# Last routing steps of a mixture-of-experts layer moved to other places in the order, and their padding matmuls with them

## The chip, the core and the metric

The kernel runs on one core of a Trainium2 chip. The metric is the device time of one execution in microseconds (us). Five engines work from queues of their own: PE (TensorE, matmuls; PEld is its weight load), DVE (VectorE), ACT (ScalarE), POOL (GpSimd) and SP (SyncE, which here issues nearly all transfers). They wait for each other through semaphores.

## The reference, cut to what matters

One decoder layer over 1024 tokens of width 1024, in fp32:

```python
proj = x @ w_in                              # split into 9 parts
y_a = hgrn2(hq, hf, hi, hg, ...) @ w_branch_a
y_b = sliding_window_attention(aq, ak, av, sinks) @ w_branch_b
merged = sigmoid(ga) * y_a + sigmoid(gb) * y_b
x = layer_norm(alpha * x + merged @ w_out, ln1_g, ln1_b)
# experts: best of 4 groups, then the best 2 of its 8 experts; 32 experts in all
glog = x @ w_rg + b_rg
elog_sel = (x @ w_re + b_re)[group of glog.max]
weights = softmax(glog)[group] * softmax(top2(elog_sel))
y[t] = sum over the 2 experts e of t:  weight * (silu(x @ w_gate[e]) * (x @ w_up[e])) @ w_down[e]
x = layer_norm(alpha * x + y, ln2_g, ln2_b)
```

## The kernel before

The work falls into four stretches: projections and attention, the recurrence, the mixing with `w_out`, the norm and the router (`mixing`, to about 811 us), and the loop over 32 experts (`moe`, 820 to about 1430 us) with the last norm. Every fp32 product is made of three matmuls on split operands: each operand is cast to fp32r on ACT (`h`, line 94), and DVE subtracts the cast from the original to get the rest (`l`, line 95). `mm3` then issues lines 99 (h with h), 100 and 101.

**The mixing stretch** is written out in ticks, two for each of 32 blocks `main`. A block's first half runs in an even tick, its second half in the odd one. Blocks 24 to 31 project the token tiles 4 to 7 with `w_out`, two column halves c each, 24 matmuls a block. What follows a tile (norm, router) is entered for later ticks. The router works on two tiles at a time (a batch) in five steps: `turn` (transposes, line 910, copied by ACT, line 912), `logits` (line 919, copied by ACT with the bias, line 920), `choose` (transposes on line 935, then a chain of small DVE operations that ends in `asg`, line 955), `place` (ranks on PE, lines 975 and 977, then DVE lines 981 to 997 up to `rat`) and `enter` (line 1004, into one table in PSUM). `BATCHES` holds for each batch the distance in ticks from a tile's norm to each step. `choose`, `place` and `enter` come last in their tick. `warm` issues matmuls on constants that nobody reads, so many in a tick as `WARM` says; each shows as two rows in the trace. After the last tick `slots` turns the table into indices (line 1018), issues the first two gathers and 20 more such matmuls; then all engines branch on a count (line 1297), and `moe` begins.

**The expert loop** streams the weights in pieces of 512 KB, 12 an expert: four of `w_g`, four of `w_u`, four of `w_d`; the order is `w_g` and `w_u` of expert e+1, then `w_d` of expert e. Piece n is loaded into an `er` tile by `fetch`, cast by ACT to `eh` and subtracted by DVE to `el` (`halve`) three pieces ahead of PE, and used in six matmuls by `piece`. `turn_x` transposes the gathered tokens of an expert (line 1097) and splits them into `xh` and `xl`; `turn_h` transposes the product of the two first layers (line 1115). Both write into the same two PSUM banks `pb`, so `turn_h` must wait until DVE has made `xl` from a bank. The order of instructions on each engine is that of the code.

All `er`, `eh` and `el` tiles, and the tiles of `w_out` before them, come from one pool of 36 buffers (`NQ`). The addresses in the built program show that buffers are handed out in the order in which they came free. A new tile waits for the last reader of the tile that had its buffer.

How many pieces are loaded ahead of the loop is set by the mixing stretch: ten are fetched in blocks 24 to 30, and then `fetch(True)` runs at the end of every tick from 62 on, four times at two ticks and twice at each later one, up to `NRAW` = 29 in all. In the loop each piece fetches one more, so this distance stays.

```python
            if tick >= 2 * len(main) - 1:
                for _ in range(4 if tick < 2 * len(main) + 1 else 2):
                    self.fetch(True)
```

Of the kernel before, what the change touches and what calls it, by code (L numbers as in the profile page):

```python
# [57 lines left out]
class Builder:  # L58
# [52 lines left out]
            for _ in range(n):  # L111
                self.nc.tensor.matmul(ps[:, 0:128], self.c("ident"), self.c("ident"), start=True, stop=True)

    WARM = {63: 11, 66: 15, 67: 5}

    def pe_order(self):
        return self.tc.manual_schedule(engines={mybir.EngineType.PE})
# [602 lines left out]
    def mixing(self):  # L720
# [84 lines left out]
        def norm(b, i, t, mv):  # L805
            for c in range(2):
                self.scale(t, mv, g1, b1, c)
            self.at(b + 2 * (i < 7), lambda: store(i, t))
            batch = next(g for g in self.BATCHES if i in g[0])
            if i == batch[0][0]:  # L810
# [8 lines left out]
        def store(i, t):  # L819
            for d in (self.x1d, self.zd):  # L820
                nc.sync.dma_start(d[i * 128:i * 128 + 128, :], t)
# [26 lines left out]
        while tick < 2 * len(main) or stages or self.late_stages:  # L848
# [15 lines left out]
            for fn in self.late_stages.pop(tick, []):  # L864
                fn()
            self.warm(self.WARM.get(tick, 0))
            tick += 1
# [23 lines left out]
    def small(self, n, nm, bufs=1):  # L891
        return self.tile([128] + (list(n) if isinstance(n, tuple) else [n]), F32, "r" + nm, bufs)

    BATCHES = ((0, 1), (4, 5, 6, 10, 14)), ((2, 3), (4, 5, 6, 10, 14)), ((4, 5), (2, 3, 4, 8, 9)), ((6, 7), (2, 3, 3, 4, 5))

    def router(self, batch):

# [536 lines left out]
```

## Time and profile before

| | |
|---|---|
| median of 3 runs | 1482.07 us (1479.93 to 1483.83) |
| time of the profiled execution | 1479.16 us |
| its span, first to last instruction | 1477.3 us |
| busy in the span: PE, PEld, DVE, ACT, POOL | 95%, 79%, 71%, 55%, 12% |
| mean granted TensorE clock | 0.988 of full speed |

The busy shares are means over stretches of different kinds. A matmul's end is modelled in these profiles, and matmuls overlap, so a busy PE is not PE at its peak; a pause of PE is nevertheless a pause.

### The profile page before, as it was taken

To read this page: it belongs to the slowest core of one execution; us is meant where nothing else is said; L and a number is where in the kernel's file an instruction comes from. 1 tells how busy PE (TensorE), PEld (TensorE's weight loads), DVE (VectorE), ACT (ScalarE), POOL (GpSimd) and SP (SyncE) were. 2 spreads that over 40 slices of the span, in tenths; PEclk is the share of its full clock that TensorE was granted. 3 is DMA by queue.
4 is the path that set the end of the run, shared out by engine and by line. 5 is a ranking of instruction groups with operands and counts; after the bars stand their busy time and mean duration, and the time that the engine had idled before them with its cause. 6 is when DMAs were issued, how large, how long until landed. Compare 5 with 4: busy or idle time off the path is not lost. (4 is left out here: it accounts for less than half of the span.)

```text
span 1477.3 us, 21008 instructions
## 1 busy us (share of the span) xinstructions
PE 1400.5 (95%) x7466; PEld 1172.5 (79%) x7466; DVE 1055.1 (71%) x1680; ACT 811.3 (55%) x1236; POOL 183.3 (12%) x137
## 2 busy tenths in 40 slices
PE   7999999999999999999997999999999999999992
PEld 5888899998888888788787877777777777777771
DVE  3266654647656764867645788888888888888978
ACT  3367434324443443313101777787777777877865
POOL 0000000000000000410000111111111111111125
PEclk9999999999999999999998999999999999999997
DMA  6124322344334323874538799999999999999643
GB/s 227 57 87 141 110 72 79 101 136 131 101 107 150 93 93 100 251 238 150 204 139 320 274 350 348 355 350 352 352 361 353 358 353 355 356 361 368 232 153 114
DMA packets 157726, 326.17 MB, mean 221 GB/s; under 512 B 18421, under 2 KB 79093, under 8 KB 157616
## 3 DMA queue, kind: packets, MB, share of 16 engines
q1 hardware_dynamic: 148688, 308.78, 58.2%
q0 software_dynamic: 8928, 16.00, 4.5%
q8 instruction: 60, 0.98, 0.3%
q14 instruction: 50, 0.41, 0.1%
HBM read 289.86 MB, written 51.38 MB: 231 GB/s over the span
## 5 line engine op out<-in xcount | busy, mean ns | idle before, releaser
L95 DVE TENSOR_TENSOR el<-er,eh 128x1024 fp32r<-128x1024 f32 x384 | 464.5, 1222 | 73.3 <-ACT eh L94 42.5
L94 ACT CAST eh<-er 128x1024 fp32r<-128x1024 f32 x384 | 395.5, 1050 | 105.2 <-PE mm L100 54.1
L100 PE MATMUL mm<-el,xh 128*128 128x512 f32 x512 | 202.9, 396 | 0.0
L101 PE MATMUL mm<-eh,xl 128*128 128x512 f32 x512 | 202.6, 396 | 0.0
L99 PE MATMUL mm<-eh,xh 128*128 128x512 f32 x512 | 201.5, 393 | 0.0
L99 PE MATMUL mm<-xh,wh 128*128 128x512 f32 x480 | 198.5, 414 | 0.0
L101 PE MATMUL mm<-xh,wl 128*128 128x512 f32 x480 | 188.7, 393 | 0.0
L100 PE MATMUL mm<-xl,wh 128*128 128x512 f32 x480 | 186.9, 389 | 0.0
L99 PEld LDWEIGHTS mm<-eh,xh 128*128 128x128 f32 x512 | 96.1, 188 | 23.6
L100 PEld LDWEIGHTS mm<-el,xh 128*128 128x128 f32 x512 | 96.1, 188 | 23.5
L101 PEld LDWEIGHTS mm<-eh,xl 128*128 128x128 f32 x512 | 96.1, 188 | 22.5
L101 PEld LDWEIGHTS mm<-xh,wl 128*128 128x128 f32 x480 | 90.0, 188 | 20.4
L99 PE MATMUL mm<-eh,hth 128*128 128x512 f32 x256 | 105.4, 412 | 0.7 <-ACT hth L94 0.7
L99 PEld LDWEIGHTS mm<-xh,wh 128*128 128x128 f32 x480 | 90.4, 188 | 15.4 <-DVE xl L95 0.4
L100 PEld LDWEIGHTS mm<-xl,wh 128*128 128x128 f32 x480 | 90.6, 189 | 14.7
L101 PE MATMUL mm<-eh,htl 128*128 128x512 f32 x256 | 101.3, 396 | 0.0
L100 PE MATMUL mm<-el,hth 128*128 128x512 f32 x256 | 100.2, 391 | 0.0
L1037 POOL DMA_INDIRECT xg<-x1d,gi x32 | 55.7, 1739 | 310.6 <-PE pb L1097 282.5
L1041 POOL DMA_INDIRECT zd<-y,gi x30 | 58.5, 1950 | 197.1 <-ACT y L1166 179.9
L99 PE MATMUL mm<-wh,xh 128*128 128x256 f32 x256 | 74.1, 290 | 0.0
L101 PE MATMUL mm<-wh,xl 128*128 128x256 f32 x256 | 72.4, 283 | 0.0
L100 PE MATMUL mm<-wl,xh 128*128 128x256 f32 x256 | 72.4, 283 | 0.0
(248 smaller groups left out, 2536.3 us busy)
## 6 DMA issues: line engine op xcount, KB each, us to landing
er<-w_g SPq DMA_DIRECT2D x128, 512.0 KB, 6.9
er<-w_u SPq DMA_DIRECT2D x128, 512.0 KB, 5.6
er<-w_d SPq DMA_DIRECT2D x128, 512.0 KB, 7.3
wr<-w_in SPq DMA_DIRECT2D x38, 512.0 KB, 4.7
gated<-st SPq DMA_DIRECT2D x32, 256.0 KB, 2.1
st<-gated SPq DMA_DIRECT2D x32, 256.0 KB, 3.3
x<-x SPq DMA_DIRECT2D x8, 512.0 KB, 9.3
wab<-w_a SPq DMA_DIRECT2D x16, 256.0 KB, 4.1
```

The costliest lines, as they stand in the source:

```text
L94: self.nc.scalar.copy(hi, src)
L95: (eng or self.nc.vector).tensor_sub(lo, src, hi.bitcast(F32))
L99: mm(out, lh, rh, start=start, stop=False)
L100: mm(out, lh, rl, start=False, stop=False)
L101: mm(out, ll, rh, start=False, stop=stop)
L1037: self.nc.gpsimd.indirect_dma_start(self.xg[e % 2], None, self.x1d, bass.IndirectOffsetOnAxis(ap=self.gi[:, e:e + 1], axis=0), bounds_chec ...
L1041: self.nc.gpsimd.indirect_dma_start(self.zd, bass.IndirectOffsetOnAxis(ap=idx, axis=0), y, None, bounds_check=T - 1, oob_is_err=False, com ...
```

## The change

Two tables change. The batch of tiles 4 and 5 does `place` and `enter` two ticks sooner, which puts them inside the last block of `w_out`; the batch of tiles 6 and 7 does all its steps one tick sooner; and the padding matmuls are spread over four ticks (31 of them before, 35 now).

```diff
-    WARM = {63: 11, 66: 15, 67: 5}
+    WARM = {63: 11, 65: 5, 66: 14, 67: 5}
...
-    BATCHES = ((0, 1), (4, 5, 6, 10, 14)), ((2, 3), (4, 5, 6, 10, 14)), ((4, 5), (2, 3, 4, 8, 9)), ((6, 7), (2, 3, 3, 4, 5))
+    BATCHES = ((0, 1), (4, 5, 6, 10, 14)), ((2, 3), (4, 5, 6, 10, 14)), ((4, 5), (2, 3, 4, 6, 7)), ((6, 7), (1, 2, 2, 3, 4))
```

On PE, at the last block of `w_out` (rows 99 to 101 on `mh` and `ml` are its matmuls; `rasg` and `rsum` belong to `place` of tiles 4 and 5, row 919 to `logits` of tile 6):

```order
 L919 MATMUL pa<-rxT,wr 36x128 x8
-L112 MATMUL mm<-const 128x128 x11
 L975 MATMUL pa<-rasg,const 128x32
 L977 MATMUL pa<-rsum,const 128x32
 L975 MATMUL pa<-rasg,const 128x32
 L977 MATMUL pa<-rsum,const 128x32
+L99 MATMUL mm<-h,mh 128x512
+L100 MATMUL mm<-l,mh 128x512
+L101 MATMUL mm<-h,ml 128x512
```

The second half of the last block (twelve matmuls, of which three are shown) stood ahead of these rows and now follows them. In the built program the first row of line 975 waits for ACT as well as for DVE, because ACT's copy of the logits reads the same bank.

On PE just behind it, from `enter` of tiles 4 and 5 through `turn`, `logits` and `choose` of tile 7 (`u` is the normed tile):

```order
 L1004 MATMUL tb<-rpay,rat 128x64 x4
+L112 MATMUL mm<-const 128x128 x11
 L910 MATMUL pb<-const,u 128x128 x8
-L112 MATMUL mm<-const 128x128 x15
+L112 MATMUL mm<-const 128x128 x5
 L919 MATMUL pa<-rxT,wr 36x128 x8
 L935 MATMUL pa<-const,rlT 128x36 x2
-L112 MATMUL mm<-const 128x128 x5
+L112 MATMUL mm<-const 128x128 x14
```

The real steps keep their order; most of the padding behind `turn` moved: eleven matmuls stand ahead of `turn` now, and fourteen instead of five behind the transposes of `choose`. On DVE, `place` of tiles 4 and 5 (lines 981 to 997) moves in the same way from behind the last tile's norm (lines 875 to 883) to ahead of its second half's addition (line 797).

The batch of tiles 6 and 7 ends one tick sooner, so there is one tick less at whose end pieces are fetched: 28 are under way ahead of the loop instead of 29. SP's queue has one load less ahead of the branch and one more behind it. With that, the buffers that the tiles of the loop take are others. On ACT, one expert's casts around its `xh`, before, with what each waits for beside its load:

```order
L94 CAST eh<-er 128x1024 [waits DMAHW2_49,DVE_49]
L94 CAST eh<-er 128x1024 [waits DMAHW3_49,PE_49]
L94 CAST eh<-er 128x1024 [waits DMAHW4_49,DVE_49]
L94 CAST xh<-pb 128x512 [waits DMASW3_49,PE_49]
L94 CAST xh<-pb 128x512 [waits PE_49]
```

and in the changed program:

```order
L94 CAST eh<-er 128x1024 [waits DMAHW2_49,DVE_49,PE_49]
L94 CAST eh<-er 128x1024 [waits DMAHW3_49,DVE_49,PE_49]
L94 CAST eh<-er 128x1024 [waits DMAHW4_49,DVE_49,PE_49]
L94 CAST xh<-pb 128x512 [waits DMASW3_49,PE_49]
L94 CAST xh<-pb 128x512 [waits PE_49]
```

The addresses tell which tile had the buffer. Before, the cast of piece n usually takes the buffer of the raw piece n-2, and the subtraction that of the `el` of n-4, which PE must have used; but once an expert, at the first piece of `w_g` (the second row above), the cast itself takes the `el` of n-4. That is the first piece of `w_d` of the expert before. Now the cast of piece n usually takes the buffer of the `eh` of n-5, and the subtraction that of the raw piece n-2; at the first piece of `w_g` the cast takes the `eh` of n-5 too, and the subtraction the `el` of n-4.

On DVE, the same place before (the second row belongs to the first piece of `w_g`):

```order
L95 TENSOR_TENSOR el<-er,eh 128x1024 [waits DMAHW2_49,PE_49,Activation_49]
L95 TENSOR_TENSOR el<-er,eh 128x1024 [waits DMAHW3_49,DVE_49,Activation_49]
L1153 TENSOR_TENSOR hh<-hh,mm 128x512 [waits PE_49]
L95 TENSOR_TENSOR el<-er,eh 128x1024 [waits DMAHW4_49,PE_49,Activation_49]
L95 TENSOR_TENSOR xl<-pb,xh 128x512 [waits DMASW5_49,Activation_49]
```

and now:

```order
L95 TENSOR_TENSOR el<-er,eh 128x1024 [waits DMAHW2_49,DVE_49,Activation_49]
L95 TENSOR_TENSOR el<-er,eh 128x1024 [waits DMAHW3_49,PE_49,Activation_49]
L1153 TENSOR_TENSOR hh<-hh,mm 128x512
L95 TENSOR_TENSOR el<-er,eh 128x1024 [waits DMAHW4_49,DVE_49,Activation_49]
L95 TENSOR_TENSOR xl<-pb,xh 128x512 [waits DMASW5_49,Activation_49]
```

The wait for PE has moved from the usual subtraction to the one at the first piece of `w_g`.

## Rows read from the trace of the kernel before

**Rows 1.** Busy time by engine in one expert's stretch; last PE clock, DMA share, GB/s.

```profile
core 0: us, PE busy (x) PEld busy (x) DVE busy (x) ACT busy (x) POOL busy (x), PEclk, DMA share, GB/s
900.00:919.20 19.20, 18.33 (x85) 14.79 (x84) 16.75 (x17) 15.29 (x18) 3.55 (x2) 1.00 0.98 366
```

**Rows 2.** Who waited for whom, expert loop (820 to 1400): total, times, longest.

```profile
ACT eh L94 <- PE mm L100: 54.1, 33, 1.8
...
PE pb L1115 <- DVE xl L95: 25.3, 29, 0.9
```

**Rows 3.** Timeline of one expert: start, us, engine, line; in brackets idle and releaser.

```profile
1042.11 0.63 PE L1115 MATMUL pb<-const,hh 128*128 128x128 f32 x4 [0.87 <-DVE xl L95]
...
1056.08 0.39 PE L100 MATMUL mm<-el,hth 128*128 128x512 f32 x1
...
1056.51 2.00 ACT L94 CAST eh<-er 128x1024 fp32r<-128x1024 f32 x2 [1.80 <-PE mm L100]
...
1057.58 1.23 DVE L95 TENSOR_TENSOR el<-er,eh 128x1024 fp32r<-128x1024 f32 x1 [1.17 <-ACT eh L94]
...
1058.41 1.06 ACT L94 CAST xh<-pb 128x512 fp32r<-128x512 f32 x2
...
1059.33 1.22 DVE L95 TENSOR_TENSOR el<-er,eh 128x1024 fp32r<-128x1024 f32 x1
...
1060.02 0.40 PE L101 MATMUL mm<-eh,htl 128*128 128x512 f32 x1
...
1060.46 1.28 DVE L95 TENSOR_TENSOR xl<-pb,xh 128x512 fp32r<-128x512 f32 x2
...
1061.29 0.63 PE L1115 MATMUL pb<-const,hh 128*128 128x128 f32 x4 [0.87 <-DVE xl L95]
```

**Rows 4.** Timeline of the routing's end and the way to the loop.

```profile
783.20 1.94 PE L919 MATMUL pa<-rxT,wr 128*36 128x128 f32 x16
...
785.24 0.36 ACT L920 ACTIVATE rlT<-pa,br 36x128 f32<-36x128 f32 x1 [4.00 <-PE pa L919]
...
787.63 0.31 PE L975 MATMUL pa<-rasg,const 128*128 128x32 f32 x2
787.70 0.75 DVE L883 SCALAR_TENSOR_TENSOR u<-u,lmv,ln_b 128x512 f32<-128x512 f32 x1
...
790.87 1.69 PE L1004 MATMUL tb<-rpay,rat 128*128 128x64 f32 x8 [2.26 <-DVE rat L997]
...
792.35 1.92 PE L910 MATMUL pb<-const,u 128*128 128x128 f32 x8
...
794.06 3.78 PE L112 MATMUL mm<-const 128*128 128x128 f32 x30
...
797.77 1.94 PE L919 MATMUL pa<-rxT,wr 128*36 128x128 f32 x16
...
805.31 0.64 PE L975 MATMUL pa<-rasg,const 128*128 128x32 f32 x2 [3.53 <-DVE rasg L955]
...
807.26 0.35 DVE L989 TENSOR_TENSOR rrr<-roh,pa 128x64 f32<-128x64 f32 x2 [0.50 <-PE pa L977]
...
808.44 0.87 DVE L997 TENSOR_SCALAR rat<-const,rank 128x128 f32<-128x128 f32 x4
...
810.78 0.19 DVE L1018 TENSOR_SCALAR gi<-tb 128x32 int32<-128x32 f32 x1 [1.47 <-PE tb L1004]
...
810.93 6.69 PE L112 MATMUL mm<-const 128*128 128x128 f32 x40
...
817.92 1.20 PE L1097 MATMUL pb<-const,xg 128*128 128x128 f32 x8 [0.30 <-PEq L1297]
```

**Rows 5.** Stretches of the routing, columns as in rows 1.

```profile
790.00:795.00 5.00, 4.13 (x23) 4.14 (x24) 1.40 (x9) 1.17 (x2) 0.00 (x0) 0.66 0.98 324
...
799.00:801.00 2.00, 1.55 (x14) 1.24 (x12) 0.39 (x3) 0.36 (x1) 0.00 (x0) 1.00 1.05 422
...
805.00:806.00 1.00, 0.69 (x4) 0.69 (x4) 0.94 (x7) 0.64 (x2) 0.00 (x0) 0.50 1.02 406
```

**Rows 6.** Transfers in the twenty experts from 900 to 1283.6.

```profile
DMA packets 40380, 136.01 MB, mean 355 GB/s; under 512 B 7236, under 2 KB 7236, under 8 KB 40353
```

## Prediction

> **What bounds the kernel now.** I read the busy shares by stretch first, then who waits for whom in the expert loop, then the timeline of one expert, and the timeline of the routing last, because the diff only speaks of the routing while its side effect lies in the loop.
>
> In the loop PE is busy for 18.33 of every 19.2 us [rows 1], more than DVE (16.75) or ACT (15.29). It is the bound, with one pause an expert: 29 times, 25.3 us in all, `turn_h` (line 1115) waits for DVE's `xl` [rows 2]. One expert takes 19.18 us, from 1042.11 to 1061.29 [rows 3].
>
> Why is `xl` late? Read the rows of one expert backwards. `xl` (1060.46) follows on DVE the subtraction at 1059.33 without a pause, and before it comes the one at 1057.58, which had waited 1.17 us for ACT. ACT's cast (1056.51) had waited 1.80 us for PE's line 100 at 1056.08 [rows 3]. That is the once-an-expert case in which a cast takes the buffer of the `el` four pieces back. So a matmul holds ACT, ACT holds DVE, and DVE holds PE.
>
> In the routing's end PE, DVE and ACT wait in turns, and nothing hides them: PE idles 2.26 us before line 1004, 3.53 us before line 975, and DVE waits for PE for 0.50 and 1.47 us [rows 4]. TensorE's granted clock is 0.66 on average in 790 to 795 and 0.50 in 805 to 806 [rows 5]: after each of these two pauses it went from 2.4 to 1.2 GHz.
>
> **The routing, step by step.** The last block's second half now stands behind `logits` of tile 6 and `place` of tiles 4 and 5. `place` must wait for ACT's copy of the logits: 785.24 + 0.36 - 783.20 = 2.40 us after line 919 starts [rows 4]; its eight rows take about 0.85 us (787.63 and on, four groups at some 0.2). So the last tile's norm comes about 3.3 us later: `u` is ready at 787.70 + 0.75 + 3.3 = 791.75 instead of 788.45. DVE does its `place` while PE is at the second half, 2.8 us of matmuls, so it adds nothing. SP's stores of the last tile, and the eleven loads queued behind them (ten now), also start 3.3 us later; they are for pieces that PE needs 18 or more pieces later, over 25 us, which covers it.
>
> What it saves: before, `turn` of tile 7 started at 792.35, 3.9 us after `u`, since `place` on DVE and line 1004 came first; now at once. It ran at the lower clock (1.7 us to the next row); at the higher one its second half needs about 0.5, the first half being ready sooner. Behind it stood 30 padding rows, 3.7 us; ten rows at 3.78 / 30 = 0.126 take 1.3 [rows 4]. From `u` to the logits: 797.77 - 788.45 = 9.3 before, 1.8 now. Less the 3.3, this gains **4.2 us**.
>
> `choose` is unchanged, but 28 padding rows (3.5 us) now cover the pause before line 975, which leaves 1.4 us of 3.53 + 1.4. If the clock holds, the ranks come before DVE needs them: **0.5 us** [rows 4]. The last entry, 808.44 + 0.87 = 809.31 to 810.78, is 1.47 us at the lower clock; four matmul rows and their drain at the higher one need about 0.45: **1.0 us**. The 40 padding rows ahead of the branch shrink from 6.69 to 5.0 us; PE goes on right behind them (817.92). This gains between nothing, if the gather or the other engines' branch ends last, and 1.65; I take **0.5**, since the gather can only start with the indices. Sum **6.2 us**, between 3 (the clock falls in the remaining pauses) and 7.5.
>
> The four additional padding matmuls are in these sums.
>
> **The loop.** With 28 pieces under way the free list is one longer, and the buffers shift. At the first piece of `w_g` the cast now waits for a piece that PE finished a whole piece (1.4 us) sooner, so ACT is out of the chain. DVE's subtraction waits for line 100 itself: 1056.08 + 0.39 = 1056.47, instead of starting at 1057.58 behind ACT, 1.1 us sooner. From that subtraction to line 1115 the rows show 1061.29 - 1057.58 = 3.71 us of DVE work [rows 3], so line 1115 can start at 1060.2. PE is free one matmul pitch (0.23) after 1060.02, at 1060.25. The pause closes.
>
> Does something else come late? `xh` must be there when `xl` starts, now about 1059.4. The second cast at 1056.51's place takes the `eh` of the first `w_d` piece and may start when PE's line 101 behind 1056.08 ends, about 1056.7; one cast is about 1.0, half of `xh` 0.53 [rows 3]: 1058.3, over 1 us to spare. All casts now wait for PE five pieces back; cast and subtraction (1.05 + 1.22) fit into the four pieces (5.6 us) left, with 3.3 us for what is between.
>
> An expert thus gets shorter by 0.87 us (the pause as the profile counts it, from the modelled end of a matmul) to 1.04 us (1061.29 - 1060.25, from the pitch). I take 0.95, the middle, for 29 pauses: **27.5 us**, with 25.3 and 30.2 as ends. If the margin of 0.04 us is missed by 0.2, 5.8 less.
>
> Sum: 6.2 + 27.5 = 33.7 us. The profiled execution would go from 1479.16 to 1445.5. It lies 2.9 us below the median of the runs, so the median goes from 1482.07 to **1448.4 us**.
>
> **A rule against it.** The loop moves 136.01 MB in twenty experts, 6.80 MB each, at a mean of 355 GB/s [rows 6], with a DMA share of 0.98 [rows 1]. At 18.2 us an expert it must move 374 GB/s. The stretch 799 to 801, plain loads alone, moved 422 GB/s at a share of 1.05 [rows 5], so there is room above 355. Were there none, an expert would stay at 6.80 / 355 = 19.16 us.
> The Trainium skill, DMA: Bandwidth & Descriptors, section Specifications, states that HBM gives one core about 358 GB/s; by that an expert would take an estimated 19.0 us and the loop gain only some 5. The 422 GB/s of [rows 5] disagree with it.
>
> **The rivals.**
> - *The transfers hold the loop.* For it: the share of 0.98. If the mixture with gathers and accumulating stores allows no more than the 366 GB/s of [rows 1], an expert takes 6.80 / 366 = 18.6 us, and the gain is 29 x 0.58 + 6.2 = 23: **1459 us**; at the mean of 355 it is 29 x 0.02 + 6.2 = 6.8: **1475 us**. Against it: [rows 5], and the lead of 28 pieces, which a slower stream first has to use up.
> - *Only the routing gets faster*, because another wait keeps `xl` late: 1482.07 - 6.2 = **1475.9 us**. For it: DVE is busy for 16.75 of 19.2 us and has little room. Against: the chain above.
> - *The clock falls in the routing's pauses again.* About 3 us of the 6.2 go: **1451.6 us**.
> - *Slower.* Casts are queued in order on ACT, and each now waits for PE five pieces back. If the one ahead of `xh` started more than 2.1 us after 1056.7, `xl` would be later than it is now, and each us beyond that costs 29 us over the loop. One us beyond: 1482.07 + 29 - 6.2 = **1505 us**. Against it: that piece's last matmul follows 1056.08 by 0.23 us in the row.
>
> **How the numbers follow.** Forecast (the pause closes, whole or nearly) 0.72, with its own range 1443 to 1456, in which the clock's rival (0.08 beside it) lies too; transfers 0.09 (1459 to 1475); routing only 0.06; slower 0.05. The low end is the sum of both upper bounds, 7.5 + 30.2, with the median's own spread of some 2 us: 1443. At the upper end the range takes in the transfers' milder case and a missed margin, to 1464. Left out are the harder transfer limit, the routing alone, the slower case and some of both tails, together about 0.2. What a measurement of this kernel can tell from no change is about 0.3%, 4.4 us. Faster by more: all cases but slower and half of the routing-only: 0.91; same 0.04; slower 0.05.
>
> **What would show it.** In the changed profile: line 1115's wait for `xl` is gone from the loop's waits or under 0.2 us each; the waits of `eh` for line 100 go to line 101; one expert takes 18.1 to 18.4 us. In the routing, the last `logits` starts about 4.2 us sooner, the indices (line 1018) 5.7 sooner, the first expert matmul about 6, and the clock stays at 1.00 from 795 on. I am wrong if line 1115 still waits, if PE waits for `eh` or `el` elsewhere, or if ACT and DVE wait for `er` loads all through the loop.

## The result and the profile after

The changed kernel takes 1444.96 us (median of 5 runs, 1443.97 to 1445.66); the kernel before, beside it, 1481.84 us (1479.93 to 1483.83). The ratio is 0.9752 (95% interval 0.9738 to 0.9766): 36.9 us less. Forecast were 1448.4 us, with a range from 1443 to 1464.

Where did the time go? Three instructions split the span: the last addition ahead of any moved step (line 797 of tile 6), and the first and the last `turn_h` (line 1115). Their rows in the timeline of the kernel before (start, us, engine, line):

```profile
768.91 0.69 DVE L797 SCALAR_TENSOR_TENSOR u<-xr,mm 128x512 f32<-128x512 f32 x1 [4.92 <-PE mm L101]
...
836.66 0.60 PE L1115 MATMUL pb<-const,hh 128*128 128x128 f32 x4
...
1425.08 0.66 PE L1115 MATMUL pb<-const,hh 128*128 128x128 f32 x4 [0.78 <-DVE hh L1153]
```

and in that of the changed kernel:

```profile
770.60 0.69 DVE L797 SCALAR_TENSOR_TENSOR u<-xr,mm 128x512 f32<-128x512 f32 x1 [4.92 <-PE mm L101]
...
833.02 0.60 PE L1115 MATMUL pb<-const,hh 128*128 128x128 f32 x4
...
1391.33 0.66 PE L1115 MATMUL pb<-const,hh 128*128 128x128 f32 x4 [0.78 <-DVE hh L1153]
```

Up to line 797 this execution was 1.69 us longer, where nothing is changed. From there to the first line 1115 it took 67.75 us before and 62.42 after, 5.33 less; from the first to the last 588.42 and 558.31, 30.11 less; behind that 52.2 in both. So 1.69 - 5.33 - 30.11 = -33.75, the difference of the spans (1477.3 and 1443.5) but for rounding. All routing times below are corrected by the 1.69.

**The loop.** The waits of 820 to 1400 in the changed kernel (total, times, longest):

```profile
ACT eh L94 <- PE mm L101: 75.3, 224, 0.8
DVE el L95 <- ACT eh L94: 29.6, 128, 1.5
...
DVE el L95 <- PE mm L100: 8.0, 27, 0.3
PEld pb L1115 <- DVE xl L95: 6.3, 30, 0.6
```

PE's 25.3 us behind `xl` [rows 2] are gone. What is left is a weight load (PEld) that waits 0.2 us an expert. The timeline of one expert shows the chain:

```profile
1023.20 1.23 DVE L95 TENSOR_TENSOR el<-er,eh 128x1024 fp32r<-128x1024 f32 x1 [0.30 <-PE mm L100]
1023.37 1.05 ACT L94 CAST eh<-er 128x1024 fp32r<-128x1024 f32 x1 [0.34 <-PE mm L101]
1024.33 1.07 ACT L94 CAST xh<-pb 128x512 fp32r<-128x512 f32 x2
...
1024.94 1.22 DVE L95 TENSOR_TENSOR el<-er,eh 128x1024 fp32r<-128x1024 f32 x1
...
1026.07 1.28 DVE L95 TENSOR_TENSOR xl<-pb,xh 128x512 fp32r<-128x512 f32 x2
...
1026.89 0.60 PE L1115 MATMUL pb<-const,hh 128*128 128x128 f32 x4
```

Read it beside [rows 3]. The subtraction at the first piece of `w_g` waits for line 100 itself, not for ACT behind line 100. From its start to line 1115 it takes 1026.89 - 1023.20 = 3.69 us (3.71 before), and line 1115 no longer waits. An expert takes 18.13 us instead of 19.18, a difference of 1.05.

**The routing.** The changed kernel's timeline:

```profile
784.21 0.36 ACT L920 ACTIVATE rlT<-pa,br 36x128 f32<-36x128 f32 x1 [2.14 <-PE pa L919]
...
784.62 0.41 PE L975 MATMUL pa<-rasg,const 128*128 128x32 f32 x2 [0.51 <-ACT rlT L920]
...
792.95 0.75 DVE L883 SCALAR_TENSOR_TENSOR u<-u,lmv,ln_b 128x512 f32<-128x512 f32 x1
...
795.52 1.94 PE L919 MATMUL pa<-rxT,wr 128*36 128x128 f32 x16
...
803.06 0.41 PE L975 MATMUL pa<-rasg,const 128*128 128x32 f32 x2 [1.51 <-DVE rasg L955]
...
807.07 0.19 DVE L1018 TENSOR_SCALAR gi<-tb 128x32 int32<-128x32 f32 x1 [0.61 <-PE tb L1004]
...
813.32 1.20 PE L1097 MATMUL pb<-const,xg 128*128 128x128 f32 x8 [1.54 <-DMA xg<-x1d,gi]
...
816.28 1.29 DVE L95 TENSOR_TENSOR xl<-pb,xh 128x512 fp32r<-128x512 f32 x2 [5.12 <-SPq L1297]
...
817.02 0.50 PE L101 MATMUL mm<-eh,xl 128*128 128x512 f32 x1 [0.70 <-DVE xl L95]
```

Against [rows 4], the last norm ends 3.6 us later (792.95 - 1.69 against 787.70), the last `logits` start 3.9 sooner (795.52 - 1.69 against 797.77), the indices 5.4 sooner (807.07 - 1.69 against 810.78), and the first transposes of the loop 6.3 sooner (813.32 - 1.69 against 817.92). Behind them PE waits 0.70 us for the first `xl`. The granted clock in three stretches of it (columns as in [rows 1]):

```profile
790.00:795.00 5.00, 3.65 (x32) 3.28 (x31) 3.19 (x6) 1.02 (x2) 2.71 (x3) 1.00 0.27 109
795.00:800.00 5.00, 4.55 (x40) 4.12 (x39) 1.53 (x9) 0.72 (x3) 0.00 (x0) 1.00 0.98 329
...
805.00:810.00 5.00, 4.40 (x39) 4.21 (x39) 4.39 (x15) 1.14 (x2) 1.57 (x1) 1.00 1.02 411
```

PEclk is 1.00 where [rows 5] had 0.66 and 0.50.

### The profile page after: what moved, and what is told of

Read it like the earlier page. It is cut to its first block, busy times and chain, and to the rows that moved or that the text cites. A ratio compares the mean times of both kernels' runs of the same rounds, so it can differ in the third digit from the quotient of the medians.

```text
span 1443.5 us, 20972 instructions
## 1 busy us (share of the span) xinstructions
PE 1394.9 (97%) x7474; PEld 1171.2 (81%) x7474; DVE 1053.2 (73%) x1680; ACT 814.8 (56%) x1236; POOL 164.7 (11%) x137
## 5 line engine op out<-in xcount | busy, mean ns | idle before, releaser
L94 ACT CAST eh<-er 128x1024 fp32r<-128x1024 f32 x384 | 401.5, 1051 | 83.9 <-PE mm L101 75.3
L1037 POOL DMA_INDIRECT xg<-x1d,gi x32 | 35.2, 1101 | 310.4 <-PE pb L1097 276.1
```

Of the source, the lines that this page charges most:

```text
L94: self.nc.scalar.copy(hi, src)
L1037: self.nc.gpsimd.indirect_dma_start(self.xg[e % 2], None, self.x1d, bass.IndirectOffsetOnAxis(ap=self.gi[:, e:e + 1], axis=0), bounds_chec ...
```

## The experiments

The theory is that the buffers did it: one load fewer ahead of the loop lengthens the free list of the pool (buffers minus pieces under way, 36 - 29 = 7 before, 8 after), and that shifts which tile's buffer each cast and subtraction takes over. Rivals are the reordered routing steps themselves, and the number of transfers under way.

**28 pieces, nothing else.**

```diff
-    NRAW = 29
+    NRAW = 28
```

> The kernel before with 28 pieces loaded ahead of the loop instead of 29; both tables stay as before. Buffer theory (one load fewer shifts which buffer each tile of the loop gets, and that takes the PE pause out of every expert): about 30 us faster than before, some 1452 us, one expert 18.1 us, line 1115 no longer behind the subtraction xl, the routing unchanged. Routing theory (the gain comes from the reordered steps): no change, 1482. Transfer theory (the gain needs a clearer DMA queue ahead of the branch): a few us at most, and the pause in each expert stays.

Measured: 1451.08 us against 1480.56, ratio 0.9800 (0.9782 to 0.9817), and 18.13 us an expert. Of PE's pause at line 1115 this is left:

```profile
PE pb L1115 <- DVE xl L95: 0.4, 2, 0.2
```

Four fifths of the gain come with the routing of before.

**Both tables, 29 pieces.** To the changed kernel:

```diff
-                for _ in range(4 if tick < 2 * len(main) + 1 else 2):
+                for _ in range(4 if tick < 2 * len(main) + 1 else 3):
```

> The changed kernel with one more fetch in each of the last ticks, so that 29 pieces are under way again; both tables as changed. Buffer theory: only the routing's 5.4 us of the trace are left, about 1476 us, and line 1115 waits for xl again 29 times, 0.9 us each, 19.2 us an expert. Routing theory: about 1445 as the changed kernel.

Measured: 1476.92 us against 1480.56, ratio 0.9977 (0.9964 to 0.9990). The waits of its loop are again those of [rows 2]:

```profile
PE pb L1115 <- DVE xl L95: 25.3, 29, 0.9
```

The reordered steps alone give 3.6 us (4.7 in the trace, from line 797 to the first line 1115). The two parts, 29.5 and 3.6 us, add up to 33.1; both changes together gave 36.9 in the first measurement and 34.5 in the second (below).

**28 pieces of 35 buffers.** To the kernel before, `NQ = 35` and `NRAW = 28`: the loads of the first experiment, but a free list of 7.

> The kernel before with 28 pieces ahead, as the first, but with 35 buffers instead of 36, so that the free list is as long as before. Buffer theory: no gain, 1482 us within 0.3%, the pause in each expert is there as before, although the loads are those of the first run. If the number of loads under way itself is what helps (less in the queue, fewer transfers in each other's way): about 1452 as the first.

Measured: 1483.15 us against 1480.56, ratio 1.0021 (1.0010 to 1.0032). Its loop:

```profile
PE pb L1115 <- DVE xl L95: 25.3, 29, 0.9
```

So it isn't the number of loads under way. The loss of 2.6 us fits what is lost ahead of the loop, in the mixing stretch, which takes its tiles from the same pool: between the additions on line 797 that the kernel before makes at 668.5 and 737.8 us, both runs with 35 buffers take 72.0 us, those with 36 take 69.2 to 69.3.

**27 pieces of 35 buffers.** `NQ = 35` and `NRAW = 27`, a free list of 8.

> 35 buffers and 27 pieces ahead, the rest as before: the free list is as long as in the changed kernel. Buffer theory: about 1452 us, 18.1 us an expert, as the first. If what counts is the absolute number of buffers, or if the smaller lead lets PE wait for loads: 1482 or slower.

Measured: 1455.99 us, ratio 0.9836 (0.9822 to 0.9849), 18.13 us an expert. Of PE's pause this is left:

```profile
PE pb L1115 <- DVE xl L95: 1.9, 3, 1.2
```

It is 4.9 us slower than 28 pieces of 36 buffers. In the traces 2.8 us are the same loss in the mixing stretch, and 1.7 come near the end of the loop, where two experts take 19.46 and 18.86 us.

**30 pieces.** To the kernel before, `NRAW = 30` and one more fetch in each of the last ticks, a free list of 6.

> The kernel before with 30 pieces loaded ahead instead of 29 (one more fetch in each of the last ticks), both tables as before. Buffer theory: the free list is one shorter, most casts now wait for PE four pieces back instead of for a raw piece two back, xl comes later still: the pause at line 1115 grows from 0.9 to between 1.3 and 1.8 us, so 12 to 26 us slower, 1493 to 1507. If a longer lead helps or does nothing: 1481.

Measured: 1505.03 us against 1480.82, ratio 1.0165 (1.0151 to 1.0178). The pause grows:

```profile
PE pb L1115 <- DVE xl L95: 45.4, 28, 1.6
```

Three lengths of the list: 6 gives 19.98 us an expert, 7 gives 19.18 (with 28 and with 29 pieces), 8 gives 18.13 (with 27 and with 28). The length of the list decides, and as causes of the 30 us the other two theories fall.

**27 and 26 pieces.** To the changed kernel, with nothing else changed, `NRAW = 27` (first) and `NRAW = 26` (second): a list of 9 and of 10.

> The changed kernel with 27 pieces ahead instead of 28. The free list is one longer again: casts and subtractions wait for tiles five pieces back that PE has long used. In the changed kernel the weight load of line 1115 still waits 0.2 us for xl in every expert; if that wait goes too, an expert takes some 0.16 us less and the whole 4 to 5 us less, about 1440. If PE is the bound already: 1445, no change against the changed kernel. If the smaller lead costs: slower, with waits for loads in the loop.

> The changed kernel with 26 pieces ahead. Buffer theory: as with 27 pieces, since nothing is left to free on PE's path: about 1440 us, or 1445 if PE was the bound already. If the lead matters: slower than with 27, with waits for loads behind the branch.

Measured: 1447.33 us, ratio 0.9774 (0.9761 to 0.9787), and 1447.06, ratio 0.9770 (0.9756 to 0.9784). My expectation of 1440 was wrong: an expert takes 18.13 us in both, so with the list of 8 PE is the bound already, and the weight load's 0.2 us lay beside PE's last matmul. Nor do the casts stop waiting for PE (with 27 pieces 192 times for line 100, 68.6 us); they only come early enough. With 26 pieces the smaller lead costs. The timeline's rows of line 1115 near the end read:

```profile
1316.70 0.66 PE L1115 MATMUL pb<-const,hh 128*128 128x128 f32 x4
...
1335.96 0.66 PE L1115 MATMUL pb<-const,hh 128*128 128x128 f32 x4 [0.91 <-DVE xl L95]
...
1354.90 0.66 PE L1115 MATMUL pb<-const,hh 128*128 128x128 f32 x4 [0.61 <-DVE xl L95]
```

These intervals are 19.26 and 18.94 us (18.13 and 18.16 in the changed kernel). In that stretch (1280 to 1400) casts wait for loads:

```profile
ACT eh L94 <- DMA er<-w_d: 8.5, 8, 2.1
...
ACT eh L94 <- DMA er<-w_g: 3.8, 6, 1.2
```

With 27 pieces only one interval is long (19.15 us), the third from the end. That one is no sure cost of the smaller lead: with 28 pieces the same interval is 18.16 and 18.74 in two executions of the changed kernel, and 18.13 to 19.55 in the four other runs with 36 buffers and 28 pieces whose loop has no pause. So a lead of 27 or 28 lasts just about as long as the loop. Why it shrinks is told below.

**No padding.** To the changed kernel:

```diff
-    WARM = {63: 11, 65: 5, 66: 14, 67: 5}
+    WARM = {}
```

> The changed kernel without the 35 padding matmuls of the four ticks (the 20 behind the indices stay). If the padding keeps TensorE's clock up: it falls to half in the pauses of the last routing steps, which run at the lower clock as in the trace of before, and the indices come 1 to 3 us later: 1446 to 1448. If the padding only fills PE's queue: it goes between 0 and 1 us the other way, 1444 to 1445. The loop is as in the changed kernel, 18.13 us an expert.

Measured: 1449.34 us, ratio 0.9787 (0.9772 to 0.9802). The last `logits` start 0.6 us sooner, but the indices come 2.5 us later than in the changed kernel, and the first line 1115 2.1 us later (1.4 against that kernel's second execution, below). The clock of its stretches:

```profile
795.00:800.00 5.00, 4.32 (x21) 3.02 (x19) 0.12 (x1) 0.95 (x2) 0.00 (x0) 0.58 0.98 347
...
805.00:810.00 5.00, 3.46 (x17) 3.32 (x17) 2.97 (x19) 2.69 (x3) 0.00 (x0) 0.50 1.02 413
```

In these executions the padding is worth 1.4 to 2.1 us. The medians differ by more (1449.34 us against 1444.96 and 1445.50), but they can't confirm the size: executions differ by some 2 us ahead of line 797, where nothing is changed (line 797 starts at 771.11 us here, at 770.60 and 768.94 in the changed kernel's two).

**The changed kernel again, the padding of before, and one batch alone.** The three ran on one chip.

> The changed kernel once more, beside the next two on one chip: 1445 us, within 0.3% of its first measurement.

Measured: 1445.50 us against 1480.00, ratio 0.9769 (0.9756 to 0.9782). In this execution of the same program the clock did fall:

```profile
800.00:805.00 5.00, 3.05 (x22) 2.80 (x22) 4.54 (x27) 3.03 (x4) 0.00 (x0) 0.85 1.02 412
805.00:810.00 5.00, 5.00 (x25) 5.00 (x25) 3.70 (x6) 0.00 (x0) 2.33 (x2) 0.50 0.88 339
```

The indices came 0.9 us later than in the first execution, and the first line 1115 0.7 us. Here PE stood behind the 40 padding rows ahead of the branch (6.55 us at the lower clock) and the branch itself, not behind the gather:

```profile
813.30 1.20 PE L1097 MATMUL pb<-const,xg 128*128 128x128 f32 x8 [0.30 <-PEq L1297]
```

So the padding doesn't hold the clock up every time. Five kept executions have these tables and this padding (also those with 29, 27 and 26 pieces): in 805 to 810 us three show 1.00 and two 0.50. The routing's gain is 4.7 to 5.3 us in all five.

The changed kernel with the padding table of before:

```diff
-    WARM = {63: 11, 65: 5, 66: 14, 67: 5}
+    WARM = {63: 11, 66: 15, 67: 5}
```

> The changed kernel with the padding table of before (no padding between turn and logits of tile 7, 15 matmuls behind choose, five behind the ranks). If the clock needs PE kept busy between turn and logits: it falls there and the last steps lose 1 to 3 us, 1446 to 1448. If the cover behind choose is what matters: no change, 1445, and the logits start up to 0.5 us sooner.

Measured: 1447.52 us, ratio 0.9779 (0.9765 to 0.9793). The clock stays at 1.00 up to 810. The last `logits` and the indices come 1.1 us sooner than in the changed kernel's first execution, more than I had expected. But the first transposes wait for the gather:

```profile
813.69 1.95 PE L1097 MATMUL pb<-const,xg 128*128 128x128 f32 x8 [2.65 <-DMA xg<-x1d,gi]
```

They run at the lower clock behind that wait (1.95 us, not 1.20), and the loop starts no sooner (the first line 1115 comes 62.82 us behind line 797; 62.42 and 63.09 in the changed kernel). In this execution, then, indices that came sooner did not bring the loop forward: the gather that lies between them ended last. What set the gather's end was not tried.

The kernel before with `NRAW = 28` and one batch moved:

```diff
-    BATCHES = ((0, 1), (4, 5, 6, 10, 14)), ((2, 3), (4, 5, 6, 10, 14)), ((4, 5), (2, 3, 4, 8, 9)), ((6, 7), (2, 3, 3, 4, 5))
+    BATCHES = ((0, 1), (4, 5, 6, 10, 14)), ((2, 3), (4, 5, 6, 10, 14)), ((4, 5), (2, 3, 4, 6, 7)), ((6, 7), (2, 3, 3, 4, 5))
```

> The kernel before with 28 pieces ahead and only the batch of tiles 4 and 5 moved; tiles 6 and 7 and the padding as before, so 30 padding rows still stand ahead of the last logits and ten behind choose. By the prediction's terms the last logits start about 1.4 us sooner against the first half of the last block than in the kernel before (16.8 us behind its first addition on line 797, not 18.2), the pause ahead of the ranks stays at 3 us or more, the clock falls in it, and the indices come about 1.4 us sooner: 1449 to 1450, against 1451 with the tables of before and 1445 with both tables. If moving tiles 4 and 5 alone brings the routing's whole gain: 1445. If it only delays the last norm: 1452 or more.

Measured: 1447.11 us, ratio 0.9776 (0.9763 to 0.9790), better than I had expected. The last `logits` start as soon as in the changed kernel, because `logits` of tile 6 here stay behind the last block, so `place` doesn't wait for ACT's copy of them and the last norm is delayed less. The indices come 1.3 us later than in the changed kernel, by the clock and the short cover behind `choose`, as expected. The first line 1115 comes 62.42 us behind line 797 in the changed kernel (63.09 in its second execution), 63.47 here, and 68.02 with the tables of before and 28 pieces. Nearly all of the routing's gain lies in moving tiles 4 and 5; what the rest adds is 0.4 to 1.1 us, which the medians can't resolve.

## Why the prediction was right

**The number: partly luck.** The profiled execution took 1445.36 us, where 1445.5 had been forecast. The parts agree less well: the loop gave 2.6 us more than was taken and the way to it 0.9 less, and this execution lost 1.69 us ahead of line 797, which the change doesn't touch. The median came 3.4 us under its forecast, because the 2.9 us by which the profiled execution of the kernel before lay under its median were carried over; that of the changed kernel lies 0.4 above its own.

**The loop's term: the mechanism as forecast, the size at its upper end.** Taken were 27.5 us, the middle between 25.3 (the pause that the profile counts) and 30.2 (29 times 1.04, from the pitch of the matmuls). Measured are 30.1. The interval between two line 1115 is what counts; a pause counted from the modelled end of the matmul ahead of it misses part of it. The rows named for it came: line 1115's wait is gone, casts wait for line 101 (224 times, 75.3 us) where they waited for line 100 (33 times, 54.1 us), and an expert takes 18.13 us, at the low end of the 18.1 to 18.4 forecast. The 0.04 us of margin held; a list of 9 or 10 gives no more.

**The routing's term: each step near its price, the last one nothing.** The norm came 3.6 us later (3.3), the last `logits` 3.9 sooner (4.2), the indices 5.4 sooner (5.7). For the way from there to the loop 0.5 was taken; the first line 1115 is 5.3 us sooner, so that was nought. What ended last in this execution is not the padding: PE was through the branch and waited 1.54 us for the gather, and then 0.70 for `xl`, since DVE stood behind its branch until 816.1:

```profile
L1297 ACTq COMPARE_BRANCH  x1: 50/50/50, 811.7 to 811.7; - x1
...
L1297 DVEq COMPARE_BRANCH  x1: 72/72/72, 811.8 to 811.8; - x1
...
L1297 ACTq EVENT_SEMAPHORE  x1: 17/17/17, 812.2 to 812.2; - x1
...
L1297 DVEq EVENT_SEMAPHORE  x1: 21/21/21, 816.1 to 816.1; - x1
```

**The transfers: the right verdict, half for a wrong reason.** I set the 422 GB/s of plain loads [rows 5] against the limit. The loop's means don't come near that. Over twenty experts of the changed kernel (881.82 to 1244.49):

```profile
DMA packets 38709, 130.01 MB, mean 358 GB/s; under 512 B 7031, under 2 KB 7031, under 8 KB 38681
```

PE uses 6.80 MB an expert [rows 6], but only 6.50 came in. The shortfall of 0.30 MB is 0.57 of a piece (512 KB) an expert, and it is taken from the lead, which was the second half of the argument. Up to 1300 us, loads issued and casts made, in the kernel before:

```profile
L94 ACT CAST eh<-er x305: 1029/1052/1070, 805.5 to 1299.2; 128x1024 fp32r<-128x1024 f32 x153
L1074 SPq DMA_DIRECT2D er<-w_g x112: 327/328/1184, 725.4 to 1289.3; - x112
L1074 SPq DMA_DIRECT2D er<-w_u x112: 327/328/741, 729.3 to 1296.4; - x112
L1071 SPq DMA_DIRECT2D er<-w_d x106: 327/328/1122, 779.3 to 1299.2; - x106
```

and in the changed kernel:

```profile
L1074 SPq DMA_DIRECT2D er<-w_g x116: 327/328/1928, 727.1 to 1300.0; - x116
L1074 SPq DMA_DIRECT2D er<-w_u x112: 327/328/736, 730.4 to 1287.3; - x112
L1071 SPq DMA_DIRECT2D er<-w_d x108: 327/328/1133, 781.4 to 1294.8; - x108
...
L94 ACT CAST eh<-er x324: 1028/1054/1060, 803.2 to 1299.1; 128x1024 fp32r<-128x1024 f32 x162
```

Before, 330 - 305 = 25 loads are issued ahead of the casts; after, 336 - 324 = 12, of which up to eight have not landed (`fetch` holds a load back until the one eight before it has). The loads queue up: in the same twenty experts the median time from issue to landing is 12.5 us, where it was 5.5 to 7.3 before. The loop is just about short enough to end before the lead is used up; with 26 pieces it isn't, and in some executions with 27 and 28 one expert near the end is late. Had the loop been longer, the rival "transfers hold the loop" would have been right from there on: 6.80 MB at 358 GB/s are an estimated 19.0 us an expert, and the late experts with 26 pieces took 19.26 and 18.94.
The Trainium skill, DMA: Bandwidth & Descriptors, section Specifications, gives about 358 GB/s as one core's share of HBM. The loop's mean agrees to the digit; the 422 GB/s of plain loads in [rows 5] don't, so that HBM is what holds the loop isn't shown here, only that this mixture, with at most eight pieces under way, moves no more. More of them under way were not tried.

**The other rivals.** "Only the routing" is settled by the first two runs. "Slower" is what one piece more would have been: with the list of 6, at 1505 us, the cast ahead of `xh` starts 2.5 us behind line 1097 (0.2 in the changed kernel) and `xl` comes too late. The wait is another than the one feared, though, for DVE's subtraction and not for PE:

```profile
1070.85 1.05 ACT L94 CAST eh<-er 128x1024 fp32r<-128x1024 f32 x1 [1.29 <-DVE el L95]
```

"The clock falls again" happened in two executions of five; the first line 1115 then came 62.9 and 63.1 us behind line 797, against 62.4 to 63.0 in the other three: at most 0.7 us rather than 3.

## What to carry to other kernels

When a schedule change alters how many buffers of a shared pool are held at once, look up which tile each later tile now waits for: here one load fewer moved a wait from one engine to another and was worth 30 us, some six times the reordering that caused it. Count a recurring pause between two starts of the same instruction, not from the modelled end of the one ahead. And when the engine that is the bound gets faster, compare its new rate with what the transfers deliver in that mixture; a lead hides a shortfall only until its pieces are used up.

## What the runs showed of the hardware that was not expected

Behind the branch on line 1297 DVE and SP stand still for 3.4 us (before, 815.5 to 818.9) to 4.3 us (after, 811.8 to 816.1), while ACT goes on after 0.5; with 26 pieces DVE's gap is 4.4, with 28 pieces and the tables of before 3.5. It doesn't follow the number of loads: the changed kernel's second execution, with the same 28 as its first, has 3.7. The cause was not tried.
The Trainium skill, Runtime: NRT & Kernel Launch, section Instruction fetch mechanics, says that a taken branch to code outside the fetched window waits for its page to be loaded; no run here shows whether that is it.

The same program ran its last routing steps at the full clock in one profiled execution (1.00 in 805 to 810) and at half (0.50) in another, while the medians of the two measurements, 1444.96 and 1445.50 us, differ by 0.5.
